# Seven block products for the output projection, and rotary query rows computed once, in a hybrid decoder block

## The chip, the cores and the metric

The kernel runs on one core of a Trainium2 chip. The metric is the device time of one execution in microseconds. TensorE is called PE here, its weight loads PEld, VectorE DVE, ScalarE ACT, GpSimd POOL and SyncE SP; SP issues nearly all DMAs, in order.

## What is computed

One decoder layer on a sequence of 1024 tokens with 1024 features, all in float32. Cut to what the change touches:

```python
u  = rmsnorm(h, ln_mix);  z = u @ w_in            # split into c_q, c_kv, k_rope, g_*, gate_a, gate_b
q  = (rmsnorm(c_q, norm_cq) @ w_uq).reshape(B, S, 8, 96)      # per head 64 plain + 32 rotary columns
q_nope, q_rope = q[..., :64], q[..., 64:]
q_rope = apply_rope(q_rope, cos, sin)             # [x1 cos - x2 sin, x2 cos + x1 sin]
k  = [k_nope, apply_rope(k_rope)];  q = q * 96 ** -0.5
y_a = causal_attention(q, k, v) @ w_oA;  y_b = gla(...) @ w_oB
mix = sigmoid(gate_a) * y_a + sigmoid(gate_b) * y_b
h   = h + mix @ w_out                             # the output projection, 1024 x 1024 x 1024
h   = h + (silu(u2 @ w_g) * (u2 @ w_u)) @ w_d,  u2 = rmsnorm(h, ln_ffn)
out = rmsnorm(h)
```

## The kernel before

**Number format.** Every float32 operand of a large product is kept as two tiles, a rounded high part and the rest (`split`, L117 to 119, and `split_to`, L164 and 165: ACT copies the high part, DVE or POOL subtracts it). A product is then three matmuls, high x high, high x low and low x high (`mm3`, L136 to 138). The input projection and the FFN already use the Strassen-Winograd scheme with seven products of half-size blocks instead of eight; `plus` and `minus` (L180, L181) are its sums.

**Stages, in order.** Input projection with the gated linear attention in between; latents and rotary tables (about 390 to 468 us of the span); attention (468 to 680 us); the mix (680 to 737.5 us); the output projection (737.5 to 828 us); the norms and the FFN (to the end). A scheduler orders each engine's instructions from the program text, the buffer pools and a timeline of its own, so the order on an engine is not the order of the text. Each engine runs its row strictly in that order.

**Query projection.** `latents` (L751) makes the sums of squares of the latent rows; for the query latents `q_split` (L800 to 802) splits the raw rows, scaled by the gain alone, as soon as they arrive, and the reciprocal root per token goes into the tables `tab` instead (`token_rows` and L881, L882). The power behind that root is an instruction of POOL (L99, `cqrs`). `load_uq` (L829 to 842) loads the weights of a head pair and writes them in a padded order of 128 columns per head: 64 plain, 32 rotary and the 32 rotary ones with the two halves exchanged. `qproj` (L844 to 854) multiplies them for one head and one half of the tokens: 9 matmuls of 512 columns, DVE multiplies the result by `tab` (L850), ACT and POOL split it. The keys carry the rotary rows likewise (`sel`, `krr`, L864). There are 16 such products, the first ahead of attention (L907) and 15 in it. Between the latents and attention the last 256 columns of the input projection are computed (`p_first`, `p_second`, `p_t2`, `p_t3`, `p_t4`, `p_t1`, `p_last`), which gives PE work in that stretch. Their step U2 begins with an ACT copy of a PSUM bank (L208).

**Attention.** 32 items of a head and a quarter of the queries; each has scores, a softmax on DVE and ACT, transposes, and the product with the values. Filler products of the mix (`mix_b`) stand between items.

**Mix.** `mix_a` (L1088 to 1098) takes one of 8 blocks of 128 features and one half of the tokens: 12 matmuls, DVE multiplies by the gate (L1093), POOL adds (L1094), ACT and DVE split (L1097, L1098).

**Output projection.** `out_mm` (L1148) multiplies one tile of 128 tokens by 256 columns of `w_out` over 8 blocks: 24 matmuls of 256 columns, and `out_proj` (L1154) has DVE add the PSUM tile to the residual `h_tm` (L1160). There are 8 tiles and 4 column blocks, 768 matmuls. `w_out` comes in 8 loads of 512 KB, each split by ACT and POOL. `norm` (L1162), the transposes and the splits of the FFN's operands for the first four tiles stand between its last tiles.

## Time and profile before

| | us |
|---|---|
| runs | 1496.61, 1494.80, 1490.79 (median 1494.8) |
| the profiled execution: time | 1490.3 |
| its span | 1488.6 |
| PE busy | 1438.9 (97%) |
| DVE busy | 1021.8 (69%) |
| ACT busy | 673.5 (45%) |
| POOL busy | 491.5 (33%) |
| DMA | 181.5 MB, mean 122 GB/s |

The busy time of PE counts overlapping matmuls: one of 512 columns is listed with 0.39 us, while the next one starts 0.23 us later. So a PE that is listed as busy can still wait a little between two of them.

### The profile page before, as it was taken

The page shows a single profiled execution, that of the slowest core. Times are in us where ns is not written, and L with a number is a line of the kernel's source. Part 1 is how long each engine was busy: PE and PEld are TensorE (multiplying, and loading weights), DVE is VectorE, ACT ScalarE, POOL GpSimd, SP SyncE. Part 2 cuts the span into 40 slices and gives each one's busy share as a digit, 9 for nine tenths or more (in the row PEclk, how much of TensorE's full clock was granted, in tenths as well). Part 3 has the DMA queues.
Part 4 walks back from the last instruction along what each step waited for, and adds up shares of the span by engine and source line. Part 5 has one row for each costly group of instructions (what it writes and reads, how often), then busy time and mean ns, then how long its engine had stood idle before and what let it go on. Part 6 is the DMA issues. An engine that isn't in the chain of part 4 may idle for free.

```text
span 1488.6 us, 20316 instructions
## 1 busy us (share of the span) xinstructions
PE 1438.9 (97%) x7422; PEld 1209.9 (81%) x7422; DVE 1021.8 (69%) x1453; ACT 673.5 (45%) x1333; POOL 491.5 (33%) x419
## 2 busy tenths in 40 slices
...
GB/s 237 43 116 128 114 92 147 86 79 109 146 93 59 1 44 143 104 173 282 250 77 86 85 73 105 94 104 107 99 100 106 93 106 148 398 202 94 139 158 57
DMA packets 123158, 181.51 MB, mean 122 GB/s; under 512 B 12898, under 2 KB 76915, under 8 KB 123059
## 3 DMA queue, kind: packets, MB, share of 16 engines
...
q8 instruction: 58, 0.95, 0.3%
q14 instruction: 42, 0.34, 0.1%
...
## 4 chain that ended last, share of the span: by engine, by line
PE 50%; DVE 2%; DMA 1%; ACT 0%; POOL 0%; issue 0%; SPq 0%; DVEq 0%; POOLq 0%
PE psB L136 6%; PE psB L138 6%; PE psB L137 6%; PE psA L138 5%; PE psD L138 5%; PE psD L136 5%; PE psA L136 5%; PE psA L137 5%; PE psD L137 4%; PE psy L137 1%; PE psy L138 1%; PE psy L136 1%; DMA d_h<-h 1%; DVE UT L165 0%; DMA d_a<-R 0%; DMA xr<-d_a 0%
## 5 line engine op out<-in xcount | busy, mean ns | idle before, releaser
L165 DVE TENSOR_TENSOR ws<-wr,ws 128x512 fp32r<-128x512 f32 x135 | 136.6, 1022 | 11.4 <-ACT ws L164 10.9
L164 ACT CAST ws<-wr 128x512 fp32r<-128x512 f32 x157 | 94.0, 617 | 64.8 <-DVE wr L181 31.5
L99 POOL TENSOR_TENSOR rx<-rs_m,nhalf 128x1 f32<-128x1 f32 x24 | 14.8, 620 | 252.0 <-DVE rs_m L98 250.6
L136 PE MATMUL ps_mm<-u,ws 128*128 128x512 f32 x208 | 83.7, 402 | 11.8 <-ACT st L208 9.5
L165 POOL TENSOR_TENSOR ws<-sS,ws 128x512 fp32r<-128x512 f32 x44 | 70.8, 1619 | 67.8 <-ACT ws L164 67.8
L1225 ACT COPY p<-psA 128x512 f32<-128x512 f32 x22 | 12.9, 586 | 157.4 <-PE psA L138 157.4
L137 PE MATMUL ps_mm<-u,ws 128*128 128x512 f32 x208 | 83.2, 400 | 0.0
L138 PE MATMUL ps_mm<-u,ws 128*128 128x512 f32 x208 | 82.8, 401 | 0.0
L164 ACT CAST ws<-xr 128x512 fp32r<-128x512 f32 x73 | 45.1, 620 | 76.6 <-PE psD L138 35.1
L165 DVE TENSOR_TENSOR ws<-xr,ws 128x512 fp32r<-128x512 f32 x73 | 50.1, 688 | 33.7 <-ACT ws L164 33.6
L136 PE MATMUL psB<-UT,ws 128*128 128x512 f32 x176 | 69.2, 393 | 3.3 <-ACT UT L164 3.3
L629 POOL TENSOR_TENSOR X<-E,gk 128x512 f32<-128x512 f32 x28 | 45.6, 1639 | 79.1 <-ACT E L627 37.9
L137 PE MATMUL psB<-UT,ws 128*128 128x512 f32 x176 | 69.8, 397 | 0.2 <-POOL UT L165 0.2
L137 PE MATMUL psA<-UB,ws 128*128 128x512 f32 x176 | 69.7, 396 | 0.0
L138 PE MATMUL psA<-UB,ws 128*128 128x512 f32 x176 | 69.7, 396 | 0.0
L136 PE MATMUL psA<-UB,ws 128*128 128x512 f32 x176 | 69.5, 395 | 0.0
L138 PE MATMUL psB<-UT,ws 128*128 128x512 f32 x176 | 69.4, 394 | 0.0
L180 DVE TENSOR_TENSOR st<-st,ps_mm 128x512 f32<-128x512 f32 x75 | 51.3, 684 | 20.2 <-PE ps_mm L138 17.0
L954 DVE TENSOR_TENSOR ws<-pspt,ws 128x512 fp32r<-128x512 f32 (+1 forms) x80 | 49.6, 631 | 17.1 <-ACT ws L953 16.5
L935 ACT ACTIVATE u<-pss,nb 128x128 f32<-128x128 f32 (+3 forms) x64 | 47.7, 746 | 25.1 <-DVE nb L933 16.6
L164 ACT CAST ws<-sS 128x512 fp32r<-128x512 f32 x88 | 50.3, 619 | 17.9 <-DVE sS L1201 17.9
L136 PEld LDWEIGHTS ps_mm<-u,ws 128*128 128x128 f32 x208 | 39.6, 191 | 21.2 <-ACT st L208 10.0
...
## 6 DMA issues: line engine op xcount, KB each, us to landing
...
```

Source lines behind the costliest of these rows:

```text
L99: nc.gpsimd.tensor_tensor(dst, m, nhalf[:, :n], ALU.pow)
L136: nc.tensor.matmul(ps, ah, bh, start=first, stop=False, **kw)
L137: nc.tensor.matmul(ps, ah, bl, start=False, stop=False, **kw)
L138: nc.tensor.matmul(ps, al, bh, start=False, stop=last, **kw)
L164: nc.scalar.copy(dst[:, 0], src)
L165: (lo_eng or nc.gpsimd).tensor_tensor(dst[:, 1], src, dst[:, 0].bitcast(F32), ALU.subtract)
L180: plus = lambda d, x, y: nc.vector.tensor_tensor(d, x, y, ALU.add)
L629: nc.gpsimd.tensor_tensor(X, E, k, ALU.mult)
L935: nc.scalar.activation(pt[:, 0:w], ps[:, 0:w], AF.Exp, bias=bias, accum_out=sums[h // 2][:, t, e:e + 1])
L954: nc.vector.tensor_tensor(tl[:, 0:w], ps[:, 0:w], th[:, 0:w].bitcast(F32), ALU.subtract)
L1225: nc.scalar.copy(tt[:, 0:HALF], psA)
```

## The change

Two parts are independent of each other.

**Query projection.** The rotary tables are written to DRAM (`d_rot`) when they are made, and loaded back as two tiles `tab` (cosine and sine for all partitions) after `p_second`. The query latents are normalised like the key ones, by the new function `normed`, which needs the root of the token first. A new function `rope_queries` computes the 8 x 32 rotary columns of all heads at once, before attention, between `p_t2` and `p_t3`: 2 groups of 128 columns x 2 halves of the tokens, 36 matmuls; DVE multiplies each PSUM tile by cosine and by sine, ACT and POOL split, and 8 tiles of 512 KB go to DRAM (`d_qr`). `qproj` now takes a head pair: the 2 x 64 plain columns in one product of 9 matmuls (8 products instead of 16), and the rotary rows of each head come by two DMAs of 32 rows x 1024. The items of attention are ordered by head pair, half of the tokens, head, quarter.

**Output projection.** With A the mix, cut by tokens and by features into A11, A12, A21 and A22, and B the weights cut likewise, the seven products are A11 B11, A12 B21, S2 T2, S1 T1, S4 B22, S3 T3 and A22 T4, each 4 tiles x 4 blocks x 3 = 48 matmuls of 512 columns. The S sums are made in the mix loop (two on POOL, two on DVE for each of 4 blocks), the mix takes its blocks in pairs c, c + 4, and A21 itself is not split. The T sums are made from `w_out`, which is loaded in 32 pieces of 256 KB (B11, B12, B21 and B22 twice each); T4 goes through DRAM (`d_t4`). The result is added to `h_tm` by 28 additions of 512 columns. The pool `r4` has 12 slots instead of 15, with two new pools for what no longer fits, and the operands U of the FFN are in other pools.

```diff
...
-            nc.scalar.activation(rot[:, hs], ang, AF.Sin, scale=fcol[:, 1:2])
             nc.scalar.activation(kk, ang, AF.Abs)
+            nc.scalar.activation(ang, ang, AF.Sin, scale=fcol[:, 1:2])
+            nc.sync.dma_start(d_rot[1][:, hs], ang)
             nc.vector.tensor_scalar(kk, kk, -1.0, math.pi / 2, ALU.mult, ALU.add)
-            for r in (0, 64):
-                nc.scalar.activation(rot[r:r + 32, hs], kk[r:r + 32], AF.Sin)
+            nc.scalar.activation(kk, kk, AF.Sin)
+            nc.sync.dma_start(d_rot[0][:, hs], kk)
...
+    def normed(rs, raws, g_, dst):
+        for half, ps in enumerate(token_rows(rs)):
+            for c, r in enumerate(raws):
+                cr = r[half]
+                nc.vector.scalar_tensor_tensor(cr, cr, g_[:, c:c + 1], ps, ALU.mult, ALU.mult)
+                nc.scalar.copy(dst[0][half][c], cr)
+                nc.vector.tensor_tensor(dst[1][half][c], cr, dst[0][half][c].bitcast(F32), ALU.subtract)
...
-    def q_split(c, half, cr):
-        nc.scalar.activation(cqh[half][c], cr, AF.Copy, scale=g_cq[:, c:c + 1])
-        nc.vector.scalar_tensor_tensor(cql[half][c], cr, g_cq[:, c:c + 1], cqh[half][c].bitcast(F32),
-                                       ALU.mult, ALU.subtract)
-
-    rs_q, _ = latents(0, 3, "cq", q_split)
+    rs_q, raws = latents(0, 3, "cq")
     sc_q = small.tile([P, NT], F32, name="sc_q", tag="sc_q", bufs=1)
     nc.vector.tensor_scalar(sc_q, rs_q, 96.0 ** -0.5, None, ALU.mult)
-    rq_ps = token_rows(sc_q)
+    normed(sc_q, raws, g_cq, cq_t)
...
+    def split_uq(src, n):
+
+        k = src.shape[2] * n
+        w = wslot()[:, 0:6 * k].rearrange("p (e c n) -> p e c n", e=2, c=3) if k == P else None
+        if w is None:
+            w = [t[:, 0:3 * k].rearrange("p (c n) -> p c n", c=3) for t in wtiles2()]
+        else:
+            w = [w[:, e] for e in range(2)]
+        hi, lo = (t.rearrange("p c (h n) -> p c h n", n=n) for t in w)
+        nc.scalar.copy(hi, src)
+        nc.gpsimd.tensor_tensor(lo, src, hi.bitcast(F32), ALU.subtract)
+        return w
...
+    def rope_queries(newbank):
+
+        raw = wraw(768).rearrange("p (c h n) -> p c h n", c=3, h=8)
+        for c in range(3):
+            nc.sync.dma_start(raw[:, c], w_uq[0][c * P:(c + 1) * P, :].rearrange("p (h n) -> p h n", h=8)[:, :, 64:96])
+        hi, lo = split_uq(raw, 32)
+        for half in range(2):
+            hs = slice(half * HALF, (half + 1) * HALF)
+            for g_ in range(2):
+                ps = newbank()
+                fs = slice(g_ * P, (g_ + 1) * P)
+                for c in range(3):
+                    mm3(ps, hi[:, c, fs], lo[:, c, fs], cqh[half][c], cql[half][c], c == 0, c == 2)
+                for k in range(2):
+                    t = sttile()
+                    nc.vector.tensor_tensor(t, ps, tab[k][:, hs], ALU.mult)
+                    q = wslot().rearrange("p (e n) -> p e n", e=2)
+                    nc.scalar.copy(q[:, 0], t)
+                    nc.gpsimd.tensor_tensor(q[:, 1], t, q[:, 0].bitcast(F32), ALU.subtract)
+                    nc.sync.dma_start(d_qr[g_][half][k], q.rearrange("p e n -> p (e n)").bitcast(F32))
+
+    def qproj(hp, half, wq, newbank):
         ps = newbank()
         for c in range(3):
-            mm3(ps, wq[0][:, c, h % 2, :], wq[1][:, c, h % 2, :], cqh[half][c], cql[half][c], c == 0, c == 2)
-        q32 = wraw(HALF)
-        nc.vector.tensor_tensor(q32, ps, tab[h % 2][:, hs], ALU.mult)
-        q = uslot(0).rearrange("p (e n) -> p e n", e=2)
-        nc.scalar.copy(q[:, 0, :], q32)
-        nc.gpsimd.tensor_tensor(q[:, 1, :], q32, q[:, 0, :].bitcast(F32), ALU.subtract)
-        return q[:, 0, :], q[:, 1, :]
+            mm3(ps, wq[0][:, c], wq[1][:, c], cqh[half][c], cql[half][c], c == 0, c == 2)
+        for e in range(2):
+            h = 2 * hp + e
+            t = uslot(0)
+            q = t.rearrange("p (e n) -> p e n", e=2)
+            j = h % 4 * 32
+            for k in range(2):
+                r = ROT[e].start + 32 * k
+                nc.sync.dma_start(t[r:r + 32].bitcast(F32), d_qr[h // 4][half][k][j:j + 32, :])
+            rows = PLAIN[e]
+            nc.scalar.copy(q[rows, 0, :], ps[rows])
+            nc.vector.tensor_tensor(q[rows, 1, :], ps[rows], q[rows, 0, :].bitcast(F32), ALU.subtract)
+            qps[h, half] = q[:, 0, :], q[:, 1, :]
...
+    tab = [uslot(0, F32) for k in range(2)]
+    for k in range(2):
+        nc.sync.dma_start(tab[k], d_rot[k])
...
-        for e in range(2):
-            nc.vector.tensor_tensor(tab[e][ROT[e], hs], rot[ROT[e], hs], rq_ps[half][ROT[e]], ALU.mult)
-            nc.scalar.copy(tab[e][PLAIN[e], hs], rq_ps[half][PLAIN[e]])
...
+    rope_queries(bank)
...
+    turn = [m for c in range(4) for m in (c, c + 4)]
+    fill = [(m, half) for half in range(2) for m in turn]
+
+    items = [(2 * hp + e, 2 * half + r) for hp in range(4) for half in range(2) for e in range(2) for r in range(2)]
...
+        if n == 4:
+            kproj(1, bank_pj)
+        if n % 8 == 0 and n < 24:
+            wqs[n // 8 + 1] = load_uq(n // 8 + 1)
+        if n % 4 == 0 and n < 28:
+            hp, half = divmod(n // 4 + 1, 2)
+            qproj(hp, half, wqs[hp], bank_pj)
...
+        if half == 1 and m < 4:
+            return
...
+        (a11, a21), (a12, a22) = parts(gas[c][0]), parts(gas[c + 4][0])
+        nc.gpsimd.tensor_tensor(a22, a21, a22, ALU.add)
+        nc.gpsimd.tensor_tensor(a21, a11, a21, ALU.subtract)
+        minus(a11, a22, a11)
+        minus(a12, a12, a11)
...
-        return r4.tile([P, S], dt, name=name, tag="r4", bufs=15)
-
-    h_tm = [slot(f"h{t}") for t in range(NT)]
-    for t in range(NT):
-        nc.sync.dma_start(h_tm[t], x2[t * P:(t + 1) * P, :])
+        return r4.tile([P, S], dt, name=name, tag="r4", bufs=12)
...
-    def out_mm(ps, w, t, cs):
-        half, i = divmod(t, 4)
-        ts = slice(i * P, (i + 1) * P)
-        for c in cs:
-            mm3(ps[:, 0:256], mh[half][c][:, ts], ml[half][c][:, ts], w[c][0], w[c][1], c == 0, c == KC - 1)
...
+    AM = {"A11": [(mh[0][c], ml[0][c]) for c in range(4)], "A12": [(mh[0][c + 4], ml[0][c + 4]) for c in range(4)],
+          "A22": [(mh[1][c + 4], ml[1][c + 4]) for c in range(4)]}
+    d_t4 = dram.tile([HALF, HALF], F32, name="d_t4")
+
+    def wo_raw(a, b):
+
+        raw = wraw(D)
+        for k, (r, n) in enumerate((a, b)):
+            nc.sync.dma_start(raw[:, k * HALF:(k + 1) * HALF], w_out[0][r * P:(r + 1) * P, n * HALF:(n + 1) * HALF])
+        return parts(raw)
+
+    def wo_split(x, tag, lo_eng=nc.vector):
+        t = wslot(tag).rearrange("p (e n) -> p e n", e=2)
+        split_to(t, x, lo_eng)
+        return t[:, 0], t[:, 1]
...
+    W = {k: [] for k in ("B11", "B21", "B22", "T1", "T2", "T3", "T4")}
+    for c in range(4):
+        b11, b21 = wo_raw((c, 0), (c + 4, 0))
+        W["B11"].append(wo_split(b11, "wh", nc.gpsimd))
+        W["B21"].append(wo_split(b21, "wl", nc.gpsimd))
...
+    def wo_prod(ps, a, w, first, adds, order=range(4)):
+
+        for i in range(4):
+            for c in order:
+                wo_mm(ps, a, w, i, c, first)
+            for half, k in adds:
+                hs = h_tm[half * 4 + i][:, k * HALF:(k + 1) * HALF]
+                plus(hs, hs, ps[i])
...
+    s_split("S2", lambda c: gas[c][0][:, 0:HALF], lambda: k4(F32R))
+    s_split("S1", lambda c: gas[c + 4][0][:, HALF:S], lambda: uslot(1))
+
+    for c in range(4):
+        b11, b12 = wo_raw((c, 0), (c, 1))
+        b21, b22 = wo_raw((c + 4, 0), (c + 4, 1))
+        minus(b11, b12, b11)
+        minus(b22, b22, b11)
+        W["T2"].append(wo_split(b22, "wh"))
+        W["T1"].append(wo_split(b11, "wl"))
+        nc.gpsimd.tensor_tensor(b21, b21, b22, ALU.subtract)
+        nc.sync.dma_start(d_t4[c * P:(c + 1) * P, :], b21)
+    by = [pbank("B", 4) for i in range(4)]
+    wo_prod(by, "A12", "B21", True, [(0, 0)])
+    wo_prod(bx, "S2", "T2", False, [(0, 1)])
+    s_split("S4", lambda c: gas[c + 4][0][:, 0:HALF], lambda: uslot(0))
+    for c in range(4):
+        b12, b22 = wo_raw((c, 1), (c + 4, 1))
+        W["B22"].append(wo_split(b22, "wh"))
+        minus(b12, b22, b12)
+        W["T3"].append(wo_split(b12, "wl"))
+    by = [pbank("B", 4) for i in range(4)]
+    wo_prod(by, "S1", "T1", True, [(1, 1)])
+    s_split("S3", lambda c: gas[c][0][:, HALF:S], lambda: uslot(0))
     g_ffn = gain_cols(ln_ffn[0], KC, "g_ffn")
-    w = [wout(nb) for nb in (2, 3)]
+    wo_prod(by, "S4", "B22", False, [(0, 1)])
+    xn0 = norm(0)
     for k in range(2):
-        for t in range(4):
-            out_proj(w[k], 2 + k, t)
-    xn0 = norm(0)
-    for t in range(4, 8):
-        out_proj(w[0], 2, t)
+        t4 = parts(wraw(D))
+        for j in range(2):
+            nc.sync.dma_start(t4[j], d_t4[(2 * k + j) * P:(2 * k + j + 1) * P, :])
+            W["T4"].append(wo_split(t4[j], "wh"))
+    wo_prod(bx, "S3", "T3", False, [(1, 1)])
...
+        for c in range(4):
+            wo_mm(bx, "A22", "T4", i, c, False)
+        hs = h_tm[4 + i][:, 0:HALF]
+        plus(hs, hs, bx[i])
...
```

The first place is ACT's row where the U2 copy (the copy of `ps_mm` into `st`) stands after the latents. Before:

```order
381 L801 ACTIVATE c_3659<-wc,g_cq 128x512 [waits DMAHW2_49]
382 L801 ACTIVATE c_3660<-wc,g_cq 128x512 [waits DMAHW3_49]
383 L801 ACTIVATE c_3661<-wc,g_cq 128x512
384 L745 CAST wh<-wr 128x512 [waits DMAHW5_49,DVE_49]
385 L164 CAST ws<-wr 128x512 [waits DVE_49]
386 L208 COPY st<-ps_mm 128x512
```

After:

```order
373 L167 CAST ws<-wr 128x512 [waits PE_49,Activation_49]
374 L167 CAST ws<-wr 128x512 [waits DVE_49] x2
375 L211 COPY st<-ps_mm 128x512
376 L273 ACTIVATE st<-ps_mm 128x512 [waits PE_49]
377 L794 CAST c_3663<-wc 128x512 [waits DVE_49]
```

The scaled copies of the query latents (L801) and the cast of the key-value weights (L745, which waits for a DMA) stood ahead of the copy, and now stand behind it.

The second place is DVE's row from the rotated key (`wr`, times the tables `u`) to the results of `rope_queries` (`st`), and the splits of the input projection (`ws`) behind them, after the change; `u_3914` and `u_3915` are the two tables.

```order
475 L896 TENSOR_TENSOR wr<-wr,u_3914 32x1024 [waits DMAHW4_49,DMAHW0_49]
476 L168 TENSOR_TENSOR ws<-wr,ws 128x512 [waits PE_49,Activation_49]
477 L896 TENSOR_TENSOR wr<-wr,u_3915 32x1024 [waits DMAHW5_49]
...
484 L860 TENSOR_TENSOR st<-ps_mm,u_3914 128x512 [waits DMAHW3_49,PE_49]
485 L860 TENSOR_TENSOR st<-ps_mm,u_3915 128x512 [waits DMAHW6_49]
...
490 L860 TENSOR_TENSOR st<-ps_mm,u_3914 128x512 [waits PE_49,Pool_49]
491 L860 TENSOR_TENSOR st<-ps_mm,u_3915 128x512 [waits Pool_49]
492 L168 TENSOR_TENSOR ws<-wr,ws 128x512 [waits DMAHW1_49,Activation_49]
```

Before, the same stretch read:

```order
473 L180 TENSOR_TENSOR st<-st,ps_mm 128x512 [waits DVE_49,PE_49]
474 L165 TENSOR_TENSOR ws<-wr,ws 128x512 [waits Activation_49]
475 L180 TENSOR_TENSOR st<-st,ps_mm 128x512 [waits DVE_49,PE_49]
476 L881 TENSOR_TENSOR u_3919<-rot,ps_g 64x512 [waits PE_49]
477 L881 TENSOR_TENSOR u_3919<-rot,ps_g 64x512
478 L165 TENSOR_TENSOR ws<-wr,ws 128x512 [waits Activation_49]
479 L180 TENSOR_TENSOR st<-st,ps_mm 128x512 [waits PE_49]
```

Splits of `ws` on which PE's next products wait stood among the table products; now they stand behind two loads of the tables and eight products of `rope_queries`. On SP the loads for these steps stand behind stores of the gate:

```order
153 L890 DMA u_3914<-d_rot 128x1024 [waits DMAHW4_49,PE_49]
154 L890 DMA u_3915<-d_rot 128x1024 [waits DMAHW5_49,PE_49]
155 L274 DMA d_gb<-st 128x512 [waits DMAHW6_49,Activation_49]
156 L745 DMA wr<-in_mla_w_ukv_dram 128x1024 [waits DMAHW7_49,DMAHW1_49,DVE_49]
157 L274 DMA d_gb<-st 128x512 [waits DMAHW0_49,Activation_49]
158 L274 DMA d_gb<-st 128x512 [waits Activation_49]
159 L849 DMA wr<-in_mla_w_uq_dram 128x8x32 [waits DMAHW7_49,DMAHW2_49,DVE_49]
```

These rows are those of after; the table loads wait for PE (their slots hold operands of `p_first`), and the rotary weights (`in_mla_w_uq`, L849) wait behind three stores that wait for ACT.

The third place is DVE's row in the output projection. Before, it held little but the additions to the residual `h`:

```order
771 L1098 TENSOR_TENSOR u_7180<-v_7106,u_7180 128x512 [waits Activation_49]
772 L1160 TENSOR_TENSOR h_7190<-h_7190,psA 128x256 [waits DMAHW2_49,PE_49]
773 L1160 TENSOR_TENSOR h_7191<-h_7191,psD 128x256 [waits DMAHW3_49,PE_49]
774 L1160 TENSOR_TENSOR h_7192<-h_7192,psB 128x256 [waits DMAHW4_49,PE_49]
```

After (`u` and `k` from `v`: split S sums; `wr` from `wr`: T sums; `ws`: split T sums):

```order
803 L183 TENSOR_TENSOR h_7254<-h_7254,psD 128x512 [waits DMAHW5_49,PE_49]
804 L183 TENSOR_TENSOR h_7255<-h_7255,psD 128x512 [waits DMAHW6_49,PE_49]
805 L168 TENSOR_TENSOR u_7529<-v_7079,u_7529 128x512 [waits Activation_49]
806 L184 TENSOR_TENSOR wr<-wr 128x512 [waits DMAHW4_49]
807 L183 TENSOR_TENSOR h_7252<-h_7252,psB 128x512 [waits DVE_49,PE_49]
808 L184 TENSOR_TENSOR wr<-wr 128x512 [waits DMAHW6_49,DMAHW5_49,DMAHW0_49]
809 L168 TENSOR_TENSOR ws<-wr,ws 128x512 [waits Activation_49]
810 L183 TENSOR_TENSOR h_7253<-h_7253,psB 128x512 [waits PE_49]
```

The additions, the S splits, the T sums and the T splits now share one row, and each waits for what stands ahead of it.

## Rows read from the trace of the kernel before

**Rows 1.** The page, parts 1 and 4: busy time by engine; chain that ended last.

```profile
PE 1438.9 (97%) x7422; PEld 1209.9 (81%) x7422; DVE 1021.8 (69%) x1453; ACT 673.5 (45%) x1333; POOL 491.5 (33%) x419
PE 50%; DVE 2%; DMA 1%; ACT 0%; POOL 0%; issue 0%; SPq 0%; DVEq 0%; POOLq 0%
```

**Rows 2.** Windows by stage: stretch and its us, busy us (instructions), granted clock, DMA.

```profile
410.80:419.50 8.70, 0.00 (x0) 0.00 (x0) 7.82 (x15) 5.72 (x10) 5.88 (x1) 0.65 0.19 60
419.50:423.70 4.20, 4.16 (x10) 3.29 (x11) 4.14 (x7) 0.18 (x1) 0.00 (x0) 0.50 0.44 125
428.00:466.00 38.00, 38.00 (x166) 31.02 (x166) 18.59 (x28) 18.03 (x37) 3.88 (x9) 1.00 0.30 100
```

**Rows 3.** Timeline 398 to 420: start, us, engine, line, tiles, [idle before <-releaser].

```profile
398.47 1.64 POOL L99 TENSOR_TENSOR ckrs<-rs_m,nhalf 128x8 f32<-128x8 f32 x1 [1.73 <-DVE rs_m L98]
...
409.81 0.95 PE L772 MATMUL ps_g<-ones,st 128*128 128x1 f32 x8
...
410.07 0.62 ACT L164 CAST ws<-wr 128x512 fp32r<-128x512 f32 x1 [0.58 <-PE ps_mm L138]
...
413.32 5.88 POOL L99 TENSOR_TENSOR cqrs<-rs_m,nhalf 128x8 f32<-128x8 f32 x1 [11.47 <-DVE rs_m L98]
413.83 0.67 DVE L165 TENSOR_TENSOR ws<-wr,ws 128x512 fp32r<-128x512 f32 x1
...
416.88 0.62 ACT L745 CAST wh<-wr 128x512 fp32r<-128x512 f32 x1 [2.08 <-DMA wr<-in_mla_w_ukv_dram]
...
418.91 0.58 ACT L208 COPY st<-ps_mm 128x512 f32<-128x512 f32 x1
...
419.54 0.79 PE L136 MATMUL ps_mm<-u,ws 128*128 128x512 f32 x1 [8.78 <-ACT st L208]
```

**Rows 4.** Timeline of PE: two matmuls of 512 columns, two of 256.

```profile
700.38 0.39 PE L137 MATMUL psy<-c,ws 128*128 128x512 f32 x1
700.61 0.39 PE L138 MATMUL psy<-c,ws 128*128 128x512 f32 x1
...
738.52 0.28 PE L136 MATMUL psA<-wh,u 128*128 128x256 f32 x1
738.63 0.28 PE L137 MATMUL psA<-wl,u 128*128 128x256 f32 x1
```

**Rows 5.** DMA issues 400 to 680: transfer, count, KB each, median us to landing.

```profile
wr<-in_mla_w_uq_dram SPq DMA_DIRECT2D x4, 288.0 KB, 2.9
```

**Rows 6.** Groups 680 to 828 by form, POOL: busy us, mean ns, idle before.

```profile
L1094 POOL TENSOR_TENSOR v<-v,k 128x512 f32<-128x512 f32 x16 | 23.7, 1494 | 6.5 <-DVE v L1093 5.1 <-issue 1.4
L119 POOL TENSOR_TENSOR wl<-wr,wh 128x1024 fp32r<-128x1024 f32 x8 | 19.8, 2484 | 34.0 <-issue 18.1 <-ACT wh L118 16.0
```

**Rows 7.** Windows: the two halves of attention, the mix, the output projection.

```profile
468.00:572.00 104.00, 102.24 (x657) 87.75 (x655) 78.66 (x127) 74.49 (x182) 29.14 (x35) 1.00 0.13 40
572.00:680.00 108.00, 104.11 (x641) 88.75 (x639) 68.88 (x112) 68.36 (x151) 34.41 (x33) 1.00 0.44 142
680.00:737.50 57.50, 57.26 (x255) 46.78 (x256) 34.69 (x42) 27.83 (x38) 41.51 (x27) 1.00 0.79 266
737.50:828.00 90.50, 90.50 (x799) 90.42 (x798) 30.13 (x59) 24.98 (x41) 21.73 (x16) 1.00 0.34 119
```

**Rows 8.** Groups 468 to 572 by form, PE: the scores of 512 columns.

```profile
L136 PE MATMUL pss<-u,u 128*128 128x512 f32 x23 | 10.2, 444 | 0.2 <-ACT u L935 0.2
L138 PE MATMUL pss<-u,u 128*128 128x512 f32 x23 | 9.1, 395 | 0.0
```

**Rows 9.** Groups 680 to 828 by form, DVE.

```profile
L1098 DVE TENSOR_TENSOR u<-v,u 128x512 fp32r<-128x512 f32 x16 | 19.8, 1239 | 11.3 <-ACT u L1097 11.3
L1093 DVE TENSOR_TENSOR v<-v,psy 128x512 f32<-128x512 f32 x16 | 10.9, 680 | 12.7 <-PE psy L138 12.7
L165 DVE TENSOR_TENSOR UB<-raw,UB 128x512 fp32r<-128x512 f32 x8 | 5.9, 761 | 1.8 <-ACT UB L164 1.8
L1160 DVE TENSOR_TENSOR h<-h,psA 128x256 f32<-128x256 f32 x14 | 5.9, 420 | 29.4 <-PE psA L138 29.2
```

155 lines of the change are left out of this document (71 added, 84 removed).

## The prediction

> **What bounds the kernel now.** I read the page first. PE is listed as busy for 97% of the span and makes up half of the chain that ended last, while no other engine has more than 2% of that chain [rows 1]. So the time is PE's row plus its waits, and a matmul that is removed is worth its pitch, unless its place is one where PE waits anyway. The pitch is read from two neighbouring starts: 0.23 us for 512 columns and 0.11 for 256 [rows 4]; I use 0.232 and 0.1135, the means over some hundred starts (38.00 us with 166 matmuls, nearly all of 512 columns, agree [rows 2]).
>
> Then I read the windows by stage. Three things are to be seen there. First, ahead of attention there is one true hole: PE does nothing from 410.8 to 419.5, and the ten matmuls behind it run at a granted clock of 0.50, that is at the lower level of 1.2 GHz [rows 2]. Second, in the first half of attention DVE and ACT are busy for 76% and 72% beside PE, in the second half for 64% and 63% [rows 7]; the first matmul of a score takes 444 ns there where the third takes 395 [rows 8], so short waits hide in the busy PE. Third, the output projection is PE alone: 90.5 of 90.5 us, DVE 30, POOL 22 [rows 7].
>
> **Part 1, the hole.** Its last releaser is ACT's copy for U2 at 418.91 [rows 3]. Ahead of it on ACT stand the scaled query latents and a cast that waits 2.08 us for a DMA [rows 3]; the order shows that both go behind the copy. The copy then follows three casts of 0.62 us from 410.07 on [rows 3], so it is done at about 412.5, and PE waits 1.7 us instead of 8.7. What is late next: 12 matmuls later PE needs the token rows, which need POOL's power `cqrs`. That instruction took 5.88 us here, while the like one for the key latents took 1.64 [rows 3]; why is not in the rows. With 1.64 PE does not wait for it. With 5.88 it ends at about 417.6, DVE then needs 1.5 us for its two followers, and PE waits 3.8 more. PE's ten slow matmuls lose 1.8 us now. The gain is 5.3 us with the long power and 9.1 with the short one; I take **-6.5**, nearer to the long one, since that is the row of this very instruction.
>
> **Part 2, new work ahead of attention.** `rope_queries` has 36 matmuls: **+8.35**. Its waits show in no row, so I bound them.
> - The tables. Their loads are issued only when PE has left their slots, and DVE's product waits for them with a split behind it that PE needs. A load of 288 KB takes 2.9 us [rows 5] and so bounds the wait from above; PE has the products of `p_second` meanwhile. 0 to 2 us, taken **+1**.
> - The rotary weights. SP issues them behind three stores that wait for ACT; then 2.9 us to land [rows 5], a cast of 768 columns, 1.5 x 0.62 = 0.9 us [rows 3], and POOL's subtraction, 0.75 x 2.48 = 1.9 us [rows 6]. The chain is 5.7 us long, and `p_t2` covers a part of it. 2 to 6 us, taken **+4**. PE's queue behind it holds all of attention's preparation, so nothing else fills this.
> - Behind it: DVE's eight products need staging slots that POOL frees at 1.5 us each [rows 6], and the splits for `p_t3` stand behind them. 1 to 4 us, taken **+2**.
>
> A wait of that length can also lower the clock, as the hole did [rows 2]; this belongs to a rival.
>
> **Part 3, attention.** 15 products of 9 become 7 of 9: 72 matmuls fewer, 72 x 0.232 = 16.7 us of PE. DVE and ACT keep their work: one product and one cast of 512 columns for a head become one subtraction and one cast of 64 x 512. Where they nearly set the pace (the first half), I count half of it; in the second half, nearly all. Four short items now follow each other at each pair's start, with little PE work to cover their softmax. The bounds are -6 and -16.7; I take **-11**. The 32 loads of query rows lie beside a DMA share of 0.13 to 0.44 [rows 7] and cost nothing unless one is late.
>
> **Part 4, the mix.** PE's work stays. POOL gets 8 more instructions of 512 columns and the low parts of B11 and B21, at 1.49 us each [rows 6], where it was busy 41.5 of 57.5 us [rows 7]. By the order its last sum ends some 12 us into the output projection; A11 B11 needs its fourth B11 after about 8 us, which POOL has at 4.6, and B21 at 11.1, which POOL has at 7.6. So **0**, with 3.5 us to spare.
>
> **Part 5, the output projection.** 768 x 0.1135 = 87.2 us become 336 x 0.232 = 78.0: -9.2. The new danger is DVE. Between the first addition and the last T2 split (needed 35 us into the stage, by PE's order) it has 11 additions of 0.68 us and 24 instructions with two operands in SBUF, in 26 us; so PE begins to wait when one of these takes more than (26 - 7.5) / 24 = 0.77 us. The rows give three prices: 0.67 with POOL little engaged [rows 3], 0.76 in the output projection with POOL busy 24% of the time, and 1.24 in the mix with POOL busy 72% [rows 7, 9]. In these 26 us POOL has some 9 us of work, 35%: between 0.85 and 0.95 us by these rows, so a wait of 2 to 4 us. I take 3, which makes **-6** for the stage, bounds -9.2 and +5 (all at 1.24: 24 x 0.47 = 11.3 us of waiting, some of it caught up).
>
> The same slowdown is what a rule of the Trainium skill says: "GPSIMD Engine Reference", section "1. Specifications", has POOL's SBUF interfaces shared with VectorE, in contention with DVE instructions that have two SBUF inputs. The trace agrees, with 0.67 us beside 1.24; by that rule every T sum and split that falls beside a POOL instruction is slow, and the stage would come out as the third rival below has it. The page gives no factor.
>
> **Part 6, the FFN.** Its matmuls stay. Fewer rotating slots and other pools move loads; I see no load that becomes late, so 0, with 3 us either way.
>
> **The sum.** -6.5 + 8.35 + 1 + 4 + 2 - 11 + 0 - 6 = -8.2 us against the profiled execution's 1490.3: 1482. The runs of before spread from 1490.8 to 1496.6 with the median 4.5 us above the profile; against the median the same sum gives 1486.6. I name **1483**, nearer to the profile, where the sum was made.
>
> **Rivals.**
> - *Everything is hidden.* The short power, the tables and weights in time, attention gets all of its 16.7 us and the output projection its 9.2. -9.1 + 8.35 + 0 + 2 + 1 - 16.7 - 9.2 = -23.7: about 1468. For it: PE's 97%. Against it: DVE and ACT at over 70% in the first half of attention.
> - *Attention is paced by the softmax.* The removed matmuls only filled waits, -6, and the new waits ahead of it are at their upper ends: -5.3 + 8.35 + 2 + 6 + 4 - 6 - 5 = +4: about 1495, no change. For it: the hidden waits of rows 8. Against it: the second half, where PE is fuller than the others.
> - *DVE bounds the output projection (slower).* One mechanism: the 24 instructions ahead of S2 T2 run beside POOL's sums, which themselves run late, and each costs more than the 0.77 us from which PE waits. At 1.24 us PE waits 11 us; if POOL's rest from the mix lies beside all of them and the S4, S3 and T3 sums (26 more) are late as well, 50 x 0.47 = 23 us. That turns -9.2 into +14, and the sum into -8.2 + 6 + 14 = +12: about 1502, and more when the fourth B21 comes late too. For it: 1.24 us in the mix. Against it: DVE idles for two thirds of this stage now, and POOL's list in it is short.
> - *The clock.* After the waits around `rope_queries` the clock falls as it did in the hole, and its 36 matmuls take twice as long, +8: the forecast becomes about 1491.
>
> **How the numbers follow.** The forecast, 1476 to 1487, has 0.45; all hidden 0.13; softmax or clock, 1487 to 1502, 0.25; DVE bound, above 1502, 0.17. What a measurement can tell from no change is 0.5%, 7.5 us about 1494.8: faster is below 1487.3, slower above 1502.3. So faster 0.58, same 0.25, slower 0.17. The range goes from 1466 (all hidden, and a little) to 1504, which leaves out the far half of the slow case.
>
> **What would show it.** In the trace of after: no idle PE of more than 4 us before the token rows (part 1; the length of `cqrs` decides). A wait of PE at the first matmul of `rope_queries`, released by POOL's subtraction, of 2 to 6 us, and a smaller one at `p_t3` (part 2). Attention shorter by 8 to 14 us (part 3). The stage from the end of the mix to the second norm some 84 us long, with PE's waits at S2 T2 released by DVE (part 5). The forecast is wrong if DVE's T splits average over 1 us, if the clock shows 0.5 around `rope_queries`, or if attention gets shorter by less than 6.

## The result and the profile after

The changed kernel takes **1516.9 us** in the median (1516.1 to 1518.4), the kernel before 1495.2 us beside it: a ratio of 1.0147 [1.0132, 1.0161]. It is slower by 22 us where a gain of 12 had been named, and it lies outside the range. The profiled execution of after took 1516.3 us with a span of 1514.6, against 1490.3 and 1488.6 before, which is 5 us under the median of before; these 26.0 us are accounted for below. One execution of `gate_late` (1619 us, granted clock 0.84, its profiled one) and one of before (2049 us) were slow throughout and enter no median and no row.

The span can be cut at the same seven events of PE in both traces. The first column of differences is measured, the last is the forecast's.

| stretch of the span, us | before | after | difference | forecast |
|---|---|---|---|---|
| start to the token rows of the query latents | 425.6 | 418.4 | -7.2 | -6.5 |
| token rows to the first score | 45.4 | 70.5 | +25.1 | +15.35 |
| first score to last score | 187.9 | 179.2 | -8.7 | -11 |
| last score to the mix's first transposes | 21.3 | 26.8 | +5.5 | (none) |
| the mix, first transposes to last product | 57.4 | 60.0 | +2.6 | 0 |
| last product to first product of the output projection | 0.2 | 12.4 | +12.2 | 0 |
| output projection | 90.7 | 84.5 | -6.2 | -6 |
| FFN, to the end | 660.1 | 662.8 | +2.7 | 0 |

The windows of after by stage follow: stretch and its us, busy us of PE, PEld, DVE, ACT and POOL (instructions), granted clock, DMA share, GB/s. They answer to [rows 2, 7].

```profile
410.80:418.40 7.60, 6.10 (x20) 4.34 (x20) 6.37 (x13) 2.40 (x5) 2.02 (x1) 0.78 0.20 71
418.40:488.90 70.50, 59.50 (x228) 45.90 (x227) 41.19 (x58) 30.53 (x52) 15.89 (x13) 0.90 0.54 179
488.90:576.00 87.10, 83.76 (x545) 71.19 (x545) 66.54 (x111) 63.76 (x144) 4.06 (x4) 0.98 0.14 43
576.00:668.10 92.10, 88.44 (x542) 75.45 (x540) 64.07 (x100) 59.77 (x133) 26.46 (x20) 0.98 0.51 160
668.10:694.90 26.80, 20.53 (x127) 17.47 (x126) 14.97 (x25) 16.19 (x30) 4.80 (x4) 0.91 0.65 214
694.90:754.90 60.00, 59.99 (x255) 49.20 (x256) 34.15 (x40) 23.20 (x37) 44.77 (x33) 0.95 0.61 204
754.90:767.30 12.40, 0.42 (x2) 0.00 (x1) 12.04 (x11) 3.71 (x7) 10.54 (x8) 0.65 0.95 361
767.30:851.80 84.50, 84.42 (x369) 68.10 (x369) 61.18 (x93) 39.10 (x69) 17.04 (x15) 0.97 0.42 139
```

The hole of [rows 2] is gone: PE is busy 6.1 of 7.6 us there. But two new stretches stand out in which PE isn't full: 11 us are missing ahead of the first score, and between the mix and the output projection PE does nothing for 12 us while DVE is busy throughout. The clock is below 1 in every row, where it was 1.00 in all of [rows 7]. The waits of PE name the releasers (total us, times, longest):

```profile
PE psA L140 <- DVE v L1127: 12.0, 1, 12.0
PE ps_mm L297 <- DVE rs_m L102: 7.5, 1, 7.5
PE acc L992 <- ACT ws L986: 4.4, 1, 4.4
PE ps_mm L140 <- ACT ws L167: 4.3, 1, 4.3
PE ps_mm L140 <- ACT wh L835: 3.8, 1, 3.8
```

The second of these, early in the kernel, is there before too (7.3 us); the other four are new. They are three places: the first product of the output projection waits for DVE's multiplication of the mix's last PSUM tile (L1127); attention's last values wait for an ACT cast (L986); and around `rope_queries` PE waits for the cast of the rotary weights (L835) and then for a split of `p_t3`'s weights (L167).

**Around the rotary products.** The rows of PE from the timeline of after (start, us, engine, line, tiles, idle before and releaser), with the middle left out:

```profile
433.62 1.02 PE L905 MATMUL ps_g<-wr,sel 64*128 64x512 f32 x2
438.40 0.80 PE L140 MATMUL ps_mm<-c,wh 128*128 128x512 f32 x1 [3.76 <-ACT wh L835]
438.99 0.63 PE L141 MATMUL ps_mm<-c,wh 128*128 128x512 f32 x1
439.42 0.63 PE L140 MATMUL ps_mm<-c,wh 128*128 128x512 f32 x1
...
444.99 0.40 PE L140 MATMUL ps_mm<-c,wh 128*128 128x512 f32 x1
445.22 0.40 PE L141 MATMUL ps_mm<-c,wh 128*128 128x512 f32 x1
...
454.10 0.50 PE L140 MATMUL ps_mm<-v,ws 128*128 128x512 f32 x1 [4.29 <-ACT ws L167]
454.44 0.39 PE L141 MATMUL ps_mm<-v,ws 128*128 128x512 f32 x1
457.05 0.79 PE L142 MATMUL ps_mm<-v,ws 128*128 128x512 f32 x1 [2.22 <-DVE ws L168]
```

PE waits 3.76 us, runs its first 14 rotary products at a pitch of 0.43 us instead of 0.23 (438.99 to 439.42), and waits again for 4.29 and 2.22 us, with slow products behind the second of these too. The windows of the two slow stretches have a granted clock (the third value from the end) of 0.54 and 0.50, so PE is at the lower level of 1.2 GHz there:

```profile
438.40:445.00 6.60, 6.60 (x17) 5.23 (x18) 0.04 (x1) 0.00 (x0) 1.82 (x1) 0.54 0.26 84
457.05:461.50 4.45, 4.45 (x11) 3.48 (x12) 1.24 (x2) 1.24 (x2) 0.00 (x0) 0.50 1.03 409
```

PE's releasers are read from ACT, DVE and POOL in the same stretch, again by the timeline (here by engine, not by time):

```profile
437.52 0.83 ACT L835 CAST wh<-wr 128x768 fp32r<-128x768 f32 x1 [0.92 <-DMA wr<-in_mla_w_uq_dram]
...
452.26 0.62 ACT L862 CAST ws<-st 128x512 fp32r<-128x512 f32 x1 [0.61 <-DVE st L860]
453.43 0.62 ACT L167 CAST ws<-wr 128x512 fp32r<-128x512 f32 x1 [0.56 <-DMA d_qr<-ws]
456.09 0.62 ACT L167 CAST ws<-wr 128x512 fp32r<-128x512 f32 x1 [2.04 <-DMA d_qr<-ws]
...
451.54 0.69 DVE L860 TENSOR_TENSOR st<-ps_mm,u 128x512 f32<-128x512 f32 x1 [0.54 <-POOL ws L863]
454.08 2.91 DVE L168 TENSOR_TENSOR ws<-wr,ws 128x512 fp32r<-128x512 f32 x1 [1.86 <-ACT ws L167]
...
446.44 10.00 POOL L863 TENSOR_TENSOR ws<-st,ws 128x512 fp32r<-128x512 f32 x8 [6.19 <-ACT ws L862]
```

The first cast waits for the load of the rotary weights. The wait of 4.29 us begins at 449.81 and has two holds, one behind the other. Until 452.88 ACT's row holds the last casts of the rotary rows; they come at the pace at which POOL's eight subtractions, without a break from 446.44 to 456.44, free the staging tiles into which DVE writes. Then the cast that PE needs waits 0.56 us more, for a store: the eight tiles of split rotary queries are taken from `wslot`, the same rotating slots that the gate's weight splits use, and this slot's store to `d_qr` lands only now.

The wait of 2.22 us is of another kind. PE has the high part of the weights and needs the low one, and DVE's subtraction for it takes 2.91 us, to 456.99, which is 0.55 us behind POOL's last subtraction. The next two of the same kind, with POOL quiet, take 0.68 and 0.69. The cast at 456.09, which waits 2.04 us for a store, falls into this time and is done at 456.71, before PE gets its low part.

### The profile page after: what moved, and what is told of

It reads as the page before. It is cut to its first block, busy times and chain, and to the rows that moved or that the text cites. A ratio compares the mean times of both kernels' runs of the same rounds, so it can differ in the third digit from the quotient of the medians.

```text
span 1514.6 us, 19625 instructions
## 1 busy us (share of the span) xinstructions
PE 1439.3 (95%) x6954; PEld 1192.2 (79%) x6954; DVE 1077.8 (71%) x1512; ACT 686.6 (45%) x1340; POOL 480.3 (32%) x403
## 4 chain that ended last, share of the span: by engine, by line
PE 61%; DVE 7%; ACT 4%; DMA 3%; issue 2%; POOL 2%; SPq 0%; DVEq 0%; ACTq 0%; POOLq 0%
PE psB L140 7%; PE psB L142 7%; PE psB L141 7%; PE psD L140 4%; PE psD L142 4%; PE psD L141 4%; PE psA L140 4%; PE psA L142 4%; PE psA L141 4%; PE ps_mm L140 2%; PE ps_mm L141 2%; PE acc L992 2%; PE ps_mm L142 2%; PE pspt L983 1%; PE pj L140 1%
## 5 line engine op out<-in xcount | busy, mean ns | idle before, releaser
L168 DVE TENSOR_TENSOR ws<-wr,ws 128x512 fp32r<-128x512 f32 x155 | 146.3, 955 | 13.3 <-ACT ws L167 12.9
L167 ACT CAST ws<-wr 128x512 fp32r<-128x512 f32 x185 | 111.3, 617 | 88.7 <-DVE wr L184 38.6
L103 POOL TENSOR_TENSOR rx<-rs_m,nhalf 128x1 f32<-128x1 f32 x24 | 14.8, 621 | 267.5 <-DVE rs_m L102 266.0
L168 POOL TENSOR_TENSOR ws<-sS,ws 128x512 fp32r<-128x512 f32 x44 | 71.0, 1625 | 68.8 <-ACT ws L167 68.8
L141 PE MATMUL ps_mm<-u,ws 128*128 128x512 f32 x208 | 83.7, 402 | 0.0
L167 ACT CAST ws<-xr 128x512 fp32r<-128x512 f32 x73 | 45.1, 620 | 78.9 <-PE psD L142 35.0
L168 DVE TENSOR_TENSOR ws<-xr,ws 128x512 fp32r<-128x512 f32 x73 | 50.1, 687 | 35.1 <-ACT ws L167 35.0
L140 PE MATMUL psB<-u,ws 128*128 128x512 f32 x176 | 69.7, 396 | 3.7 <-ACT u L167 3.7
L141 PE MATMUL psB<-u,ws 128*128 128x512 f32 x176 | 69.3, 394 | 1.7 <-POOL u L168 1.7
L140 PE MATMUL psA<-u,ws 128*128 128x512 f32 x176 | 69.4, 395 | 0.0
L142 PE MATMUL psB<-u,ws 128*128 128x512 f32 x176 | 69.3, 394 | 0.0
L142 PE MATMUL psA<-u,ws 128*128 128x512 f32 x176 | 68.9, 392 | 0.0
L141 PE MATMUL psA<-u,ws 128*128 128x512 f32 x176 | 68.2, 389 | 0.0
L992 PE MATMUL acc<-ws,v 128*128 128x256 f32 (+1 forms) x320 | 53.2, 295 | 8.1 <-ACT ws L986 4.4
L167 ACT CAST ws<-sS 128x512 fp32r<-128x512 f32 x88 | 50.3, 618 | 18.6 <-DVE sS L1228 18.6
L966 DVE TENSOR_REDUCE nb<-pss 128x1 f32<-128x128 f32 (+3 forms) x64 | 48.1, 751 | 12.9 <-PE pss L964 12.3
```

What stands on the lines that cost most here:

```text
L103: nc.gpsimd.tensor_tensor(dst, m, nhalf[:, :n], ALU.pow)
L140: nc.tensor.matmul(ps, ah, bh, start=first, stop=False, **kw)
L141: nc.tensor.matmul(ps, ah, bl, start=False, stop=False, **kw)
L142: nc.tensor.matmul(ps, al, bh, start=False, stop=last, **kw)
L167: nc.scalar.copy(dst[:, 0], src)
L168: (lo_eng or nc.gpsimd).tensor_tensor(dst[:, 1], src, dst[:, 0].bitcast(F32), ALU.subtract)
```

## Experiments

Medians are in the table at the end of this section; the kernel before beside them took 1493.8 to 1495.0 us. "Stretches" are those of the table above.

**Each half alone.** `a_only` has the seven block products and the old query path; `b_only` has the new query path and the old output projection.

> Only the output projection by seven block products; the query projection as before. The loss of the whole change lies, by the trace of after, in five places: -7 us in the hole behind the latents, +25 around the rotary queries, -10 in attention, +9 at the end of attention, +12 at the start of the output projection, -6 in it, +3 in the FFN. Theory: the +12 comes from the mix and its sums alone, so it is here too; the +9 at the end of attention needs both changes (the gates' sigmoid stands ahead of attention's last cast on ACT only where both are made). Then this run takes 1495 + 12 - 6 + 3 = 1504 us, PE waits 10 to 13 us for DVE at the first block product, and no wait of over 2 us at the end of attention. Rival: the wait at the first product is a late effect of the new attention order (DVE arrives late in the mix); then it is under 4 us here and the time is 1490 to 1494.

> Only the query projection with the rotary rows once; the output projection as before. Theory: -7 (hole) + 25 (rotary queries) - 10 (attention) = +8, so 1503 us, with PE waits of 4, 4 and 2 us around the rotary queries and none over 2 us at the end of attention. Rival: the end of attention is late because of the new order of the items alone; then that wait is here as well and the time is 1510 to 1514.

Measured: 1503.6 us and 1503.8 us, ratios 1.0053 [1.0037, 1.0069] and 1.0051 [1.0029, 1.0073]. Each half by itself loses about 9 us. In `b_only` the token rows come at 418.2 and the first score 70.2 us later, in `a_only` the first product of the output projection stands 7.7 us behind the mix: the two large losses belong to one half each. Together they cost 22, not 18; a part of the rest is the end of attention, which takes 26.8 us in after, 21.2 in `a_only`, 22.7 in `b_only` and 21.3 before.

**Whose PSUM bank.** One unused tile put first moves the accumulators of the first products off the bank that the mix's last product still holds:

```diff
+    pbank("B", 4)
     bx = [pbank("AD"[i // 2], 2) for i in range(4)]
```

> The whole change, with one PSUM tile allocated first and never used, so that the accumulators of the first block products lie in banks 4 to 7 instead of 0 to 3. In after the first of them lies in the bank of the mix's very last product, which DVE reads last. Theory: PE waits for that bank; it now waits for the last but two products' reads, and the wait of 12.0 us falls to 1 to 4 us: 1517 - 9 = 1508 us. Rival: PE waits for late operands (splits of the mix or of the weights on DVE and POOL), and the bank was only the last to be named: the wait stays over 8 us, or comes back 8 us later at the fourth block, and the time is 1514 to 1518.

Measured: 1510.2 us, 1.0102 [1.0072, 1.0131]. The wait ahead of the first product falls from 12.4 to 2.7 us, but the products then take 91.4 us instead of 84.5, with these waits of PE from 750 us on (2.4 us of the first line are the wait ahead of the first product):

```profile
PE psA L140 <- ACT ws L167: 5.5, 3, 2.6
PE psA L141 <- DVE ws L168: 2.0, 2, 1.2
```

So the bank mostly decides where PE waits. Most of the wait comes back as a wait for the split weights, whose sums and low parts stand in the same queue of DVE. What is late is DVE itself. The time is near the expected 1508, but not for the expected reason: wait and products together are only 2.8 us shorter than in after, and 5.0 of the 8.0 us between the two profiles lie ahead of the token rows, a difference of the kind told below the table.

**Why DVE is late.** DVE's rows just ahead of the first product, in after:

```profile
756.25 0.68 DVE L1127 TENSOR_TENSOR v<-v,psy 128x512 f32<-128x512 f32 x1
756.85 1.38 DVE L168 TENSOR_TENSOR k<-v,k 128x512 fp32r<-128x512 f32 x1
758.15 1.74 DVE L184 TENSOR_TENSOR wr<-wr 128x512 f32<-128x512 f32 x1
759.82 1.75 DVE L1134 TENSOR_TENSOR u<-v,u 128x512 fp32r<-128x512 f32 x1
761.49 0.67 DVE L1127 TENSOR_TENSOR v<-v,psy 128x512 f32<-128x512 f32 x1
762.09 1.15 DVE L1134 TENSOR_TENSOR u<-v,u 128x512 fp32r<-128x512 f32 x1
763.16 3.42 DVE L184 TENSOR_TENSOR v<-v,v 128x512 f32<-128x512 f32 x2
766.50 0.68 DVE L1127 TENSOR_TENSOR v<-v,psy 128x512 f32<-128x512 f32 x1
```

Every instruction with two operands in SBUF takes 1.15 to 1.75 us here, those that read one operand from PSUM (L1127) 0.67 to 0.68. POOL works beside them nearly all the time (10.54 of 12.40 us in the window above). Two ways to relieve DVE were tried. `nosum` leaves out the 16 sums of the mixed blocks (so four of the seven products multiply something else). `mix_dve` leaves nothing out and gives DVE more to do: the mix's 16 additions, 8 of the sums and the low parts of B11 and B21 go from POOL to DVE, 32 instructions:

```diff
-        nc.gpsimd.tensor_tensor(gt, gt, yb[:, half * HALF:(half + 1) * HALF], ALU.add)
+        nc.vector.tensor_tensor(gt, gt, yb[:, half * HALF:(half + 1) * HALF], ALU.add)
...
-        nc.gpsimd.tensor_tensor(a22, a21, a22, ALU.add)
-        nc.gpsimd.tensor_tensor(a21, a11, a21, ALU.subtract)
+        plus(a22, a21, a22)
+        minus(a21, a11, a21)
...
-        W["B11"].append(wo_split(b11, "wh", nc.gpsimd))
-        W["B21"].append(wo_split(b21, "wl", nc.gpsimd))
+        W["B11"].append(wo_split(b11, "wh"))
+        W["B21"].append(wo_split(b21, "wl"))
```

> The whole change, with the four S sums of each block left out of the mix (16 instructions of DVE and POOL; the block products are taken of unsummed blocks, so the result is another one). Theory: the wait of 12.4 us at the first block product comes from these sums, which stand ahead of the mix's own reads on DVE and slow each other on DVE and POOL; without them it falls under 3 us, and the S2 T2 product waits less: 1517 - 10 = 1507 us. Rival: the splits of the weights on POOL are what slows DVE; then the wait stays over 8 us: 1513 to 1517.

> The whole change, with 32 instructions of the mix moved from POOL to DVE: its 16 additions, 8 S sums and the low parts of B11 and B21. DVE then has more to do in that stretch, POOL only the splits of the mix's own weights. Theory: DVE is late in the mix since POOL and DVE slow each other on operands in SBUF (1.2 to 1.7 us for an instruction that takes 0.67 alone); with POOL nearly still, DVE's splits there fall under 0.9 us, and DVE is done earlier although it has 32 instructions more: the wait at the first block product falls under 4 us, 1517 - 9 = 1508 us. Rival: DVE is late because it has too many instructions; then the wait grows over 15 us and the time is 1518 to 1530.

Measured: `nosum` 1509.0, 1.0087 [1.0056, 1.0118], with a wait of 6.4 us; `mix_dve` 1506.3, 1.0075 [1.0058, 1.0092], with a wait of 6.2. Taking 16 instructions away and taking POOL away are worth the same 6 us at this place; both runs had been expected to bring the wait under 4 us, and half of it stayed. Of the 8.1 and 13.7 us between their profiles and that of after, 2.0 and 3.8 lie ahead of the token rows. The groups of DVE in the mix (busy us, mean ns, idle before), first of after, 694 to 768:

```profile
L1134 DVE TENSOR_TENSOR u<-v,u 128x512 fp32r<-128x512 f32 x11 | 13.4, 1220 | 3.8 <-ACT u L1133 3.8
L1127 DVE TENSOR_TENSOR v<-v,psy 128x512 f32<-128x512 f32 x16 | 10.8, 679 | 6.1 <-PE psy L142 6.0
L184 DVE TENSOR_TENSOR v<-v,v 128x512 f32<-128x512 f32 x6 | 9.8, 1629 | 0.7 <-POOL v L1158 0.6
```

and the same of `mix_dve`, 688 to 755:

```profile
L1128 DVE TENSOR_TENSOR v<-v,k 128x512 f32<-128x512 f32 x15 | 11.4, 758 | 0.1
L1127 DVE TENSOR_TENSOR v<-v,psy 128x512 f32<-128x512 f32 x16 | 10.9, 680 | 2.5 <-PE psy L142 2.5
L1134 DVE TENSOR_TENSOR u<-v,u 128x512 fp32r<-128x512 f32 x11 | 8.2, 745 | 1.4 <-ACT u L1133 1.4
L184 DVE TENSOR_TENSOR v<-v,v 128x512 f32<-128x512 f32 x4 | 2.7, 682 | 0.0
```

With POOL quiet the same instruction costs 0.68 to 0.76 us instead of 1.22 to 1.63, and DVE gets through its longer list earlier. The instructions that read PSUM cost 0.68 in both. That is the theory's side: the two engines slow each other where both of DVE's operands lie in SBUF. POOL pays as well: its subtraction on 128x512 took 1.68 us on average in the mix of after (L168) and 1.29 in that of `mix_dve` (L123). DMA traffic is not the difference, as its share was 0.67 and 0.68 in these two windows.

One by one the instructions are plainer than their means. Of DVE's 27 instructions on 128x512 with two operands in SBUF in the window of after, the 18 that began while an instruction of POOL was running took 0.98 to 1.78 us, and the other 9 took 0.68 to 0.70; in `mix_dve` 2 began so (1.36 and 1.79 us) and 50 did not (0.68 to 0.69). So these windows have two prices, beside POOL and alone, and a mean only tells how many fell beside POOL.

That the two share SBUF interfaces, and contend where a DVE instruction has two SBUF inputs, is what the Trainium skill states ("GPSIMD Engine Reference", section "1. Specifications"); these rows agree, with 1.63 beside 0.68 us.

**When the rotary rows are made.** `rope_late` moves the call behind the last gate projection; `rope_early` leaves it and only moves the loads of its weights, ahead of the latents and into a tile of their own.

```diff
     p_t2(w)
-    rope_queries(bank)
     p_t3(w)
     p_t4(w, out_gb, True)
     p_t1(w, out_gb)
     p_last(w, out_gb)
+    rope_queries(bank)
```

> The whole change, with the rotary queries after the last step of the input projection instead of between its steps t2 and t3. Theory: there was nothing between PE's last other product and the arrival of the rotary weights, and the splits that PE needed next waited for slots held by the stores of the rotary rows; both are covered here by PE's other products, and the clock stays at 1.00. Of 3.8 + 4.3 + 2.2 us of waits and 4.6 us at half clock, 12 to 15 us come back: 1502 to 1505 us. Rival: the waits move to the first products with the new queries, since their rows come back from DRAM just ahead of attention: 3 to 8 us of wait there, 1507 to 1513 us.

> The changed kernel with only the loads of the rotary weights moved ahead of the latents, into a tile of their own. Theory (the 3.8 us wait ahead of the rotary products is that load, with its split right behind it): 1517 - 4 = 1513, the waits of 4.3 and 2.2 us behind the products stay. Rival (the split on ACT and POOL stands behind other work and the wait stays, or moves behind the products): 1516 to 1518.

Measured: `rope_late` 1502.4, 1.0048 [1.0036, 1.0060]; `rope_early` 1501.4, 1.0048 [1.0034, 1.0063]. The stretch from the token rows to the first score falls from 70.5 to 57.3 and 60.3 us. For `rope_late` that was expected. For `rope_early` 4 us were expected and 15 came: 10.2 in this stretch, the rest ahead of it and at the mix. The waits of PE from 414 to 475 in `rope_early`:

```profile
PE ps_mm L140 <- ACT ws L167: 3.2, 1, 3.2
```

The wait for the weights is gone, the half-speed products behind it too (the pitch of the rotary products is 0.23 us there), and of the two waits behind them 3.2 us are left of 6.5: the second is gone, since the low part on DVE takes 0.94 us there instead of 2.91. So one load that is late by 3.8 us cost about 10. No run tells these waits from the clock, or POOL's pace from the slots held by the stores; own slots for the split queries would tell the latter, and this wasn't tried.

**The gates' sigmoid.** In after ACT's row has the table load and the first sigmoid of the mix's gates ahead of attention's last cast:

```profile
689.12 1.28 ACT L1117 ACT_TABLE_LOAD   x1 [4.64 <-DMA v<-d_ga]
690.42 1.06 ACT L1117 ACTIVATE v<-v 128x1024 f32<-128x1024 f32 x1
691.38 0.46 ACT L986 CAST ws<-pspt 128x384 fp32r<-128x384 f32 x1
```

The load of the gates is late, and the cast for which PE waits 4.4 us stands behind it. In `a_only` and `b_only` the order of ACT is the other way round, and this wait is not there. `gate_late` forces that order in after.

> The whole change, with an order put on ACT alone: the sigmoid of the gates not ahead of attention's last cast. Theory: in after that sigmoid waits 4.6 us for its DMA and for a table load with the last cast of attention behind it, PE waits 4.4 and 1.5 us and then runs some 25 matmuls at half clock; this goes, and the stretch from the last score to the first product of the mix gets 5 to 6 us shorter: 1517 - 7 = 1510 us. Rival: the DVE and POOL work of the mix sets the end of this part, not PE; then the stretch gets shorter, but the wait at the first block product grows from 12 to 16 us or more, and the time is 1514 to 1517.

Measured: 1516.9, 1.0150 [1.0132, 1.0168]: no gain. What became of the 4 us is seen in the next kernel, which has the same edit.

**All corrections.** `best1` is `rope_late`, `gate_late` and `mix_dve` together. `best3` puts the sigmoid still later, behind the last copy of the softmax sums, and writes the sums of the last two column pairs behind the first 16 groups of products.

> Three corrections together: the rotary queries after the input projection's last step, the gates' sigmoid behind attention's last cast, and the mix's additions, S sums and first weight splits on DVE. By the theory of separate causes the gains add: 1502 (rotary queries late) - 6 - 9 = 1487 us, with no PE wait over 3 us between the latents and the FFN. Rival: what is freed in one place is waited for in the next (DVE is the bound of the mix and the block products together), and the time is 1495 to 1500.

> The changed kernel with the rotary products behind the last gate projection, the gates' sigmoid behind the last copy of the softmax sums on ACT, the mix's POOL work on DVE, and the sums of the last two column pairs written behind the first products. Theory: against the run with the first three of these (1494.3) the wait of 4.2 us on that copy and 4 of the 6.1 us ahead of the first product go: 1487. Rival (the sums come back as waits between the products, as with the other banks): 1491 to 1494.

Measured: 1494.3, 1.0004 [0.9993, 1.0016], and 1494.1, 0.9999 [0.9986, 1.0012]: no difference from before, and 7 us over the expectation in both. In `best1` the sigmoid has only moved: PE now waits for the copies of the softmax sums that stand behind it on ACT.

```profile
PE psy L1061 <- ACT rb L1058: 4.2, 1, 4.2
```

In `best3` this is still 3.1 us, and the wait ahead of the first product 5.2. Both edits of order were worth little; in these rows the wait went to the next instruction of the row.

**Which part pays.** `hole` is the kernel before with one thing taken over: the query latents are normalised before they are split. `holeA` adds the output projection with the corrections of the mix, and leaves the rotary part inside every head.

> The kernel before with one thing taken over from the change: the query latents are normalised and then split, as the key latents are; the rotary part stays inside every head. Theory (the hole alone is worth its 7.2 us, and nothing behind it needs the old order): the token rows come at 418 instead of 425.6, every later stretch keeps its length, 1488 against 1495. Rival (what is won there is waited for again ahead of attention, since loads and the gates' weights then end last): 1494 to 1495.

> The output projection by seven products and the normalised latents, without the rotary rows once; the mix's 16 additions, 8 sums and two sets of low parts are on DVE instead of POOL, and the sums of the last two column pairs are written behind the first 16 groups of products. Theory (the output projection is worth its 6 us once DVE's queue is short): 1495 - 7 (hole) - 6 (products) + 2 (mix) + 4 (attention's tail, as in the run with the output projection alone) + 2 (FFN) = 1490. Rival (the wait on the mix's last read of PSUM stays at 6 us): 1496.

Measured: `hole` 1491.3, 0.9977 [0.9963, 0.9991], with the token rows at 418.4; `holeA` **1487.3**, 0.9954 [0.9938, 0.9970]. `holeA` is faster than both kernels, by 6.8 us against before; 1490 had been expected. In its trace the wait ahead of the first product is 0.8 us and the products take 83.7.

**What the rotary rows cost when their load is early.** `b_early` is `b_only` with the early load; `best4` is `best3` with the early load in the place of the late call. It differs from `holeA` by the rotary rows and the order on ACT.

> The query projection alone, with the rotary weights' load ahead of the latents. Theory (late load: 10 of the 25 us ahead of attention): 1503.8 - 11 = 1493, and against the kernel with the normalised latents alone (1491): 60 - 47 = +13 ahead of attention, 191 - 181 = -10 in it, +2 behind it in attention's tail and the mix: the rotary rows once are worth nothing or cost a little, 1491 to 1496. Rival (the forecast's sum holds once the load is early): 1487 or less.

> All corrections together: rotary weights early, the gates' sigmoid behind the last copy of the softmax sums, the mix's work on DVE, the last sums behind the first products. Theory: from the run with the early weights (1501): -2 (sigmoid) -7 (mix) = 1492, 4 to 5 over the kernel with everything but the rotary rows once (1487). Rival (the rotary rows pay once all queues are mended): 1484 or less.

Measured: `b_early` 1494.7, 1.0002 [0.9986, 1.0017]; `best4` 1498.7, 1.0037 [1.0025, 1.0049]. `b_early` is 3.5 us over `hole`. By stretches: +14.7 from the token rows to the first score (62.1 against 47.4), -10.2 in attention (181.3 against 191.5), +1.2 at its end, +1.8 in the mix and -3.5 ahead of the token rows, a difference of the kind told below the table. The 191.5 us of `hole` hold a wait of 3.3 us that is 1.2 in before; against before's 187.9 attention gives back 6.6. `best4` is 11 over `holeA`, where 5 had been expected. In the mix of `best4` one row stands out beside `holeA`:

```profile
718.54 0.69 DVE L184 TENSOR_TENSOR wr<-wr 128x512 f32<-128x512 f32 x1 [3.95 <-DMA wr<-in_w_out_dram]
```

DVE stands still for 3.95 us for a load of the output weights, with the mix's last multiplications behind it in its queue, and the first product then waits 5.9 us. In `holeA` DVE does not wait for this load, and the wait is 0.8. Why the load comes later with the rotary rows was not taken apart, and no run shows what its being early would be worth.

| kernel | median us | rows to first score | attention | its end | mix | wait | products |
|---|---|---|---|---|---|---|---|
| before | 1493.8 to 1495.2 | 45.4 | 187.9 | 21.3 | 57.4 | 0.2 | 90.7 |
| after | 1516.9 | 70.5 | 179.2 | 26.8 | 60.0 | 12.4 | 84.5 |
| `a_only` | 1503.6 | 45.5 | 192.1 | 21.2 | 59.2 | 7.7 | 88.9 |
| `b_only` | 1503.8 | 70.2 | 181.3 | 22.7 | 59.0 | 0.2 | 90.7 |
| `banks` | 1510.2 | 69.7 | 181.7 | 26.7 | 58.8 | 2.7 | 91.4 |
| `nosum` | 1509.0 | 69.7 | 181.3 | 26.5 | 59.0 | 6.4 | 83.2 |
| `mix_dve` | 1506.3 | 68.3 | 180.4 | 25.6 | 59.6 | 6.2 | 83.7 |
| `rope_late` | 1502.4 | 57.3 | 181.4 | 25.5 | 59.3 | 12.2 | 84.0 |
| `rope_early` | 1501.4 | 60.3 | 180.2 | 25.9 | 59.2 | 7.7 | 86.7 |
| `best1` | 1494.3 | 58.9 | 181.5 | 25.2 | 59.6 | 6.1 | 83.8 |
| `best3` | 1494.1 | 58.9 | 181.5 | 23.8 | 61.0 | 5.6 | 84.0 |
| `best4` | 1498.7 | 60.2 | 180.7 | 23.9 | 61.0 | 6.3 | 83.5 |
| `b_early` | 1494.7 | 62.1 | 181.3 | 22.6 | 59.2 | 0.2 | 91.0 |
| `hole` | 1491.3 | 47.4 | 191.5 | 21.4 | 57.4 | 0.2 | 90.7 |
| `holeA` | 1487.3 | 47.4 | 189.1 | 21.2 | 59.7 | 0.8 | 83.7 |

The stretch ahead of the token rows is left out of this table: it varies from 413.4 to 418.4 us among the kernels that have the new query path, also where nothing ahead of it differs. The windows show one source of it, a granted clock from 60 to 100 us that is 0.91 in after and 1.00 in `banks`, and from 260 to 300 us 0.91 and 0.96. So a difference of 5 us between two profiles there says nothing of the edit.

## Why the prediction was wrong

What failed are three terms for PE's waits, put at +7, nothing and 0 and measured at 16.8, 5.5 and 14.8 us: those around the rotary rows, at the end of attention, and behind the mix.

**Part 1, the hole: right in kind.** -7.2 against -6.5. PE waits 1.50 us for ACT's copy instead of 8.78 [rows 3], 7.3 less, so the size does not rest on the stretch that varies; and `cqrs` was the short kind this time:

```profile
411.95 2.02 POOL L103 TENSOR_TENSOR cqrs<-rs_m,nhalf 128x8 f32<-128x8 f32 x1 [7.55 <-DVE rs_m L102]
412.65 0.49 PE L140 MATMUL ps_mm<-u,ws 128*128 128x512 f32 x1 [1.50 <-ACT st L211]
```

With the short kind the working had -9.1, so the -6.5 that was taken is near by luck. The rest is the clock, which the working had at full speed behind the shorter wait: from 414.01 to 417.00 the pitch of PE's products is 0.43 us.

`hole` shows the part by itself: its token rows come 7.2 us earlier as well, but 2.0 are lost again ahead of the first score and 3.6 in attention, where a wait of PE for DVE's half of a split grows from 1.2 to 3.3 us: that half stands behind two additions of DVE that take 1.81 and 1.75 us beside POOL. 1.3 us of the span and 2.8 of the median are left. So the hole goes as forecast, and a part of what that wins is given back later in this kernel.

**Part 2, the new work ahead of attention: the terms for its waits were too small.** +25.1 against +15.35. The matmuls are right (8.35), the wait for the rotary weights has the right size (3.8 against +4, though ACT's cast released PE and not POOL's subtraction), and the tables cost nothing (0 against +1). The term "behind it" failed: 4.3 + 2.2 = 6.5 against +2 with an upper bound of 4. It counted POOL's pace in freeing staging tiles, and ACT's row did run at this pace for most of the first wait. Missing were the slots held by the stores to `d_qr`, which end that wait 0.56 us later, and DVE's low part of PE's next weights, which took 2.91 us beside POOL: the slowdown of part 4, which the prediction looked for in the output projection alone. And the clock, left to a rival, was a cost behind both waits (granted 0.54 around `rope_queries`, a sign of being wrong that the prediction had named): the 16 pitches from 438.40 to 444.99 take 6.6 instead of 3.7 us, the ten from 457.05 to 461.48 take 4.4 instead of 2.3, together 5.0 us. These five numbers, 8.35 + 3.8 + 0 + 6.5 + 5.0, make 23.7 of the 25.1.

**Part 3, attention: right in kind, 2 us short.** -8.7 against -11, and between -6.6 and -10.2 with the query projection alone (`b_early` against before and against `hole`). Of the 16.7 us of PE that were removed about half came, as the working had it for the part where the softmax nearly sets the pace. The other half of the change works against it: in `a_only`, with the old query path, attention is 4.2 us longer than before, with a wait of 4.0 us that is 1.2 in before, of the same kind as that in `hole`.

**The end of attention: not looked at.** +5.5. The prediction took the work up to the mix as part of attention and did not follow ACT's row there. The scheduler had placed the gates' sigmoid, which waits 4.64 us for its load, ahead of a cast that PE needs.

**Part 4, the mix: the step that failed most.** +14.8 against 0. It added POOL's new instructions at POOL's price and found 3.5 us to spare. DVE got work in the same stretch too, and the two engines pay for it together: DVE's sums cost 1.63 us, where [rows 9] had 1.24 for the worst kind. DVE falls behind, and with it the read of the mix's last tiles, a step that the prediction did not have on its list at all: it asked when B11 and B21 are split, not when PSUM is read out. `mix_dve` and `nosum` each bring back 6 of the 12 us, `banks` shows that the bank is only where it is felt.

**Part 5, the output projection: the right number, partly by luck.** -6.2 against -6, which was -9.2 for the matmuls and +3 for a wait on DVE at S2 T2. The matmuls are as forecast; the wait did not come. In its place PE's clock was low behind the wait of 12 us, and the first 11 products took 4.9 us instead of 2.6:

```profile
767.30:771.00 3.70, 3.67 (x9) 2.93 (x10) 1.88 (x4) 2.05 (x4) 2.25 (x2) 0.50 0.39 135
```

The splits of the weights cost 0.73 us on average in this stage, below the 0.77 from which PE would have waited, since POOL had done nearly all of its list by then:

```profile
L168 DVE TENSOR_TENSOR ws<-wr,ws 128x512 fp32r<-128x512 f32 x23 | 16.4, 730 | 0.7 <-ACT ws L167 0.7
```

The price was read off a scale, 0.85 to 0.95 us by POOL's busy share. The trace has no such scale: of the 57 instructions with two operands in SBUF in this stage 50 took 0.68 or 0.69 us, and the seven that began beside one of POOL took 1.30 to 1.79. (The row of [rows 3] that was taken for little engaged POOL stands beside `cqrs`, a POOL instruction on 128x8 that is listed busy throughout.) The third rival, slower at 1502, had the right cause and the wrong place: the slowdown struck ahead of the stage, where POOL was busy anyway.

**Part 6, the FFN: within its bound.** +2.7 against 0, 3 either way. Every kernel with the seven products has it, at 2.0 to 3.9 us, and none of the others has over 0.5.

**The sum.** The hole and the output projection are right within 1 us, both with some luck, attention within 2.3 and the FFN within 2.7, but the three places of waiting are short by 9.75, 5.5 and 14.8 us. Each rival was priced as if the others did not happen; the clock and DVE's slowdown happened at once. They were also priced from the profiled 1490.3 us, while the result is read against the median 1494.8, by which the third is about 1507. And the rotary rows paid in none of the orders tried: with their load early they cost 14.7 us ahead of attention and give back 7 to 10 in it. The forecast had +15.35 against -11, a loss as well; it hid behind the gains of the other parts, because the sum was made for the change as a whole.
